# Two-layer hybrid decoder trunk on one core: four projections with the weights as stationary operand, two factors and the skip on VectorE, the state space branch begun a chunk later

## The chip, the core and the metric

The kernel runs on one core of a Trainium2 chip. The core has five engines with an instruction stream each, which meet only through semaphores: TensorE (PE; its weight loads are PEld in the profile), VectorE (DVE), ScalarE (ACT), GpSimd (POOL) and SyncE (SP, which here only issues DMA transfers). An engine works its stream off in the order in which the program was written. Matmuls write to PSUM, eight banks of 512 float32 columns on 128 partitions. The metric is device time of one execution in microseconds.

## What is computed

Sequence 256, width 1024, two layers. Each layer is a gated feed-forward block, a mixer and a second gated feed-forward block, each between two RMS norms and added to the residual h. The mixer, to which the change is confined, is:

```python
q, k, v, z, xbc, dt_raw, u, vg, gate_raw = jnp.split(xn @ w_in, split_at, axis=-1)
y_a = moba_attention(q, k, v)                       # 8 heads x 128, causal, one block of 256
xbc = jax.nn.silu(causal_depthwise_conv(xbc, conv_w, conv_b))
xs, bm, cm = jnp.split(xbc, [SSM_WIDTH, ...])       # 1024, 256, 256 columns
y_s = ssd_scan(xs, dt, a, bm, cm) + d_skip[:, None] * xs
y_s = rms_norm(y_s * jax.nn.silu(z), ssm_norm_g)
u = jax.nn.gelu(u)
vg = layer_norm(jax.nn.gelu(vg), sgu_ln_g, sgu_ln_b)
sv = jnp.einsum('gij,bcjgd->bcigd', tril(sgu_w), vg) + sgu_b   # chunks of 128 tokens
y_c = u * sv
merged = gate0 * (y_a @ p_attn) + gate1 * (y_s @ p_ssm) + gate2 * (y_c @ p_sgu)
return merged @ w_out
```

## The kernel before

**Tiles.** Tokens are two tiles of 128 (t = 0, 1). Activations that feed a large product are kept transposed, features on partitions, in two fp32r parts (hi and lo, `xh` and `xl`). A weight block of 128 x 1024 arrives by DMA (`load`), and `split` makes its two parts: ScalarE casts `whi` (L182), VectorE subtracts for `wlo` (L183). 495 blocks pass so. `done` of a block lets the block 11 places later be split, so a split stands about ten blocks ahead of its use. The RMS factor `r2` of a token is not in x; it is multiplied in where a product leaves PSUM.

**Products.** In `gemm` a 128 x 128 piece of x is the stationary operand and 512 weight columns move: three matmuls per piece, token tile and chunk of 512 columns (L215 xh·whi, L216 xh·wlo, L217 xl·whi), 48 matmuls of 512 columns per chunk. The result has tokens on partitions. Where features are wanted on partitions, ScalarE scales the result out of PSUM (`tokens`, L482), TensorE transposes it in fours (`transposed`, L491, tile `ctr`), and ScalarE copies it out again (L494). This is done for the three chunks of xbc, two of q and two of k. u stays with tokens on partitions; its product y_c is transposed by `to_parts` (L287, `xtr`).

**Order.** One program is written by Python tasks. `pump` is called after each unit of matmuls, advances a clock by their nominal time, steps every task (`tick`) whose wait (table `W`) is over, and then issues one split. What a task issues at a step stands in the streams behind the matmuls issued so far. `finish` steps a task to its end at once. So the order on each engine is fixed by nominal times, not by when things are ready.

**The mixer's sequence** is: xbc (three chunks), z (two), the time steps `dt_task`, q0, then the state space task `ssd` is started; q1, k0, k1, v0, v1 follow, and `finish(ss)`; then attention, the gates and the three output products (`branch`), vg, u, and `sgu` inside the last gates. In `ssd`, for each token tile t and group g: two `weights` steps (matmul `seg` L655, mask add on VectorE L657, four exponentials on ScalarE L661, multiply on VectorE L663), then 8 matmuls `yd` (L686) which need both, and their addition to y and gating by z on VectorE (L689, L697). `scaled` makes y = d_skip·xs on GpSimd (L643) and xs·dt on VectorE (L646).

**Buffers.** PSUM: 5 banks `acc` for the products, 3 banks `tr` for everything else, both handed out in rotation. SBUF: 16 tiles `b4` of 4 KB per partition, 6 tiles `b2` of 2 KB.

Of the kernel before, what the change touches and what calls it, by code (L numbers as in the profile page):

```python
# [17 lines left out]
L = 2  # L18
# [22 lines left out]
G_F1, G_MX, G_F2, G_SSM, G_CW, G_CB, G_SB, G_N = 0, 8, 16, 24, 32, 80, 92, 100  # L41

RAW, SPLIT, HOLD, START, NEAR, PACE = 6, 11, 6, 2, 1, 0
B4, B2 = 16, 6
# [7 lines left out]
def trunk(ctx, tc, a):  # L52
# [49 lines left out]

    sums = cst.tile([P, 512], F32R, name="sums")
    G.memset(sums.bitcast(F32), 0.0)
# [146 lines left out]

    def chunk(key, kt=KD, n=512):
# [56 lines left out]
    class XT:  # L309
# [14 lines left out]
        def l(self, k, t):  # L324
            return self.lo[t][:, k, :]

# [119 lines left out]
    def spatial_weights(l):  # L446
        ws = b4("wsp", (P, 8, P))
        nc.sync.dma_start(ws, a["sgw"][l].rearrange("g j i -> j g i"))
        gb = row("sgu_ln_g", l), row("sgu_ln_b", l)
# [6 lines left out]
    def mixer(l, x, r2, nxt):  # L456
# [11 lines left out]
        halfr, rq = {}, {}  # L468

        def factors():  # L470
            for t in range(NT):
                halfr[t] = small("halfr", 1, bufs=4)
                G.tensor_scalar(halfr[t], r2[t], 0.5, 0.0, op0=ALU.mult, op1=ALU.add)
                rq[t] = small("rq", 1, bufs=4)
                G.tensor_scalar(rq[t], r2[t], float(HD) ** -0.5, 0.0, op0=ALU.mult, op1=ALU.add)

        def tokens(ps, scales, name):

            out = []
            for t in range(NT):  # L480
                o = b2(name)
                A.activation(o, ps[t], AF.Copy, scale=scales[t])  # L482
                out.append(o)
            return out

        def transposed(toks, place, eng):

            for t in range(NT):
                ps = tr("ctr")
                for j in range(4):  # L490
                    T.transpose(ps[:, j * P:(j + 1) * P], toks[t][:, j * P:(j + 1) * P], ident)  # L491
                p3 = ps.rearrange("p (k t) -> p k t", k=4)
                if eng == "a":
                    A.copy(place(t), p3)  # L494
                else:
                    V.tensor_copy(place(t), p3)
                yield W["tr"]
# [6 lines left out]
        def conv(c, ps):  # L504
            toks = tokens(ps, r2, "xtok")
            xc = b4("xc", (P, 4, S))
            yield W["x0"]
            yield from transposed(toks, lambda t: xc[:, :, t * P:(t + 1) * P], "a")
# [32 lines left out]
        def dt_task(wdt):  # L541
# [55 lines left out]
            for j in range(4):  # L597
                T.matmul(pr[:40, j * P:(j + 1) * P], d4[:, j, :], tri, start=True, stop=True)
            A.copy(sums[:40, :], pr[:40, :])
# [12 lines left out]
            st.update(dt=dt, nacs=nacs, eac=eac, dec=dec)  # L612
# [489 lines left out]
```

## Time and profile before

| | us |
|---|---|
| median of three runs | 1508.65 (1508.64 to 1510.26) |
| the profiled execution: its own time | 1512.7 |
| its span, first to last instruction | 1510.9 |
| PE busy in the span | 1496.5 |
| DVE busy, ACT busy | 932.5, 782.7 |
| mean granted TensorE clock | 0.996 |

The profiled execution lies 1.8 us over its span and 4 us over the median of the unprofiled runs. The mixers stand at 205 to 572 us and 955 to 1322 us of the span. TensorE is busy nearly throughout, but a matmul's end in the trace is modelled and its bar overlaps the next, so the distance from one matmul's start to the next one's start is what tells its cost.

### The profile page before, as it was taken

How to read it: one execution, taken by the hardware profiler on the slowest of the kernel's cores; microseconds unless marked ns; L12 is line 12 of the kernel's file. 1: busy time of each engine (PE TensorE's matmuls, PEld its weight loads, DVE VectorE, ACT ScalarE, POOL GpSimd, SP SyncE). 2: the span in 40 equal slices, each digit the busy share in tenths (PEclk: the TensorE clock that was granted, in tenths of full speed). 3: DMA queues.
4: the chain of work that ended last, by engine and by line, in shares of the span. 5: the costliest groups of instructions: out<-in, count | busy, mean ns of one | idle time of the engine just before them, and what ended most of it. 6: DMA issues, size and time to landing. Idle time of an engine off the chain costs nothing.

```text
span 1510.9 us, 18964 instructions
## 1 busy us (share of the span) xinstructions
PE 1496.5 (99%) x7218; PEld 1246.5 (83%) x7218; DVE 932.5 (62%) x1112; ACT 782.7 (52%) x1079; POOL 55.0 (4%) x97
## 2 busy tenths in 40 slices
PE   9999999999999999999999999999999999999998
PEld 7888888878888888888888888888788888888886
DVE  6655468666566858555475554776665677675552
ACT  6544358655374537444364443765554644464441
POOL 0000020000000000000000000200000000100000
PEclk9999999999999999999999999999999999999999
DMA  8766646335556446666566664554354665476650
GB/s 298 251 190 195 195 156 194 124 126 178 158 180 220 172 139 228 199 182 199 154 220 188 182 199 147 210 167 140 112 193 141 195 196 167 154 253 189 186 153 28
DMA packets 77914, 270.29 MB, mean 179 GB/s; under 512 B 8960, under 2 KB 12160, under 8 KB 77824
## 3 DMA queue, kind: packets, MB, share of 16 engines
q1 hardware_dynamic: 77248, 268.76, 55.6%
q8 instruction: 56, 0.92, 0.2%
q10 hardware_dynamic: 576, 0.33, 0.1%
q14 instruction: 34, 0.28, 0.0%
HBM read 268.01 MB, written 1.05 MB: 178 GB/s over the span
## 4 chain that ended last, share of the span: by engine, by line
PE 94%; DVE 4%; ACT 1%; issue 1%; POOL 0%; DMA 0%; DVEq 0%; ACTq 0%; POOLq 0%
PE gu L215 11%; PE gu L217 11%; PE gu L216 11%; PE dn L217 5%; PE dn L216 5%; PE dn L215 5%; PE br L215 3%; PE br L217 3%; PE br L216 3%; PE gate L217 2%; PE gate L215 2%; PE gate L216 2%; DVE wlo L183 2%; PE xbc L215 1%; PE xbc L217 1%; PE xbc L216 1%
## 5 line engine op out<-in xcount | busy, mean ns | idle before, releaser
L183 DVE TENSOR_TENSOR wlo<-raw,whi 128x1024 fp32r<-128x1024 f32 x495 | 601.7, 1234 | 363.0 <-ACT whi L182 362.2
L182 ACT CAST whi<-raw 128x1024 fp32r<-128x1024 f32 x495 | 513.2, 1051 | 380.0 <-PE gu L217 150.6
L215 PE MATMUL gu<-whi,xh 128*128 128x512 f32 (+1 forms) x768 | 291.6, 380 | 1.6 <-ACT xh L303 1.5
L217 PE MATMUL gu<-whi,xl 128*128 128x512 f32 (+1 forms) x768 | 287.1, 374 | 0.0
L216 PE MATMUL gu<-wlo,xh 128*128 128x512 f32 (+1 forms) x768 | 286.7, 373 | 0.0
L217 PEld LDWEIGHTS gu<-whi,xl 128*128 128x128 f32 x768 | 145.3, 189 | 26.8 <-DVE xl L304 1.1
L215 PEld LDWEIGHTS gu<-whi,xh 128*128 128x128 f32 x768 | 145.3, 189 | 26.5 <-ACT xh L303 2.0
L216 PEld LDWEIGHTS gu<-wlo,xh 128*128 128x128 f32 x768 | 145.5, 189 | 24.9 <-DVE wlo L171 0.9
L215 PE MATMUL dn<-whi,hTh 128*128 128x512 f32 x352 | 138.2, 393 | 0.0
L217 PE MATMUL dn<-whi,hTl 128*128 128x512 f32 x352 | 137.1, 390 | 0.0
L216 PE MATMUL dn<-wlo,hTh 128*128 128x512 f32 x352 | 137.1, 389 | 0.0
L217 PEld LDWEIGHTS dn<-whi,hTl 128*128 128x128 f32 x352 | 66.1, 188 | 13.8
L215 PE MATMUL gate<-whi,xh 128*128 128x512 f32 x192 | 77.3, 403 | 0.0
L216 PEld LDWEIGHTS dn<-wlo,hTh 128*128 128x128 f32 x352 | 66.2, 188 | 13.2
L215 PEld LDWEIGHTS dn<-whi,hTh 128*128 128x128 f32 x352 | 66.1, 188 | 13.2
L217 PE MATMUL gate<-whi,xl 128*128 128x512 f32 x192 | 75.0, 390 | 0.0
L216 PE MATMUL gate<-wlo,xh 128*128 128x512 f32 x192 | 74.8, 390 | 0.0
L403 ACT CAST hTh<-htr 128x512 fp32r<-128x512 f32 (+1 forms) x48 | 26.5, 551 | 47.9 <-PE htr L397 47.9
L404 DVE TENSOR_TENSOR hTl<-htr,hTh 128x512 fp32r<-128x512 f32 (+1 forms) x48 | 30.9, 643 | 29.6 <-ACT hTh L403 29.6
L303 ACT CAST xh<-xg 128x512 fp32r<-128x512 f32 (+1 forms) x25 | 15.1, 603 | 62.6 <-DVE xg L301 62.6
L217 PEld LDWEIGHTS gate<-whi,xl 128*128 128x128 f32 x192 | 36.0, 188 | 7.7
L216 PEld LDWEIGHTS gate<-wlo,xh 128*128 128x128 f32 x192 | 36.2, 188 | 6.6
(244 smaller groups left out, 2275.8 us busy)
## 6 DMA issues: line engine op xcount, KB each, us to landing
raw<-in_mix SPq DMA_DIRECT2D x232, 512.0 KB, 4.3
raw<-in_gu SPq DMA_DIRECT2D x175, 512.0 KB, 4.5
raw<-in_dn SPq DMA_DIRECT2D x88, 512.0 KB, 3.7
row_ffn_post_g<-in_ffn_post_g SPq DMA_DIRECT2D x4, 512.0 KB, 4.5
wsp<-in_sgw SPq DMA_DIRECT2D x2, 512.0 KB, 5.3
row_sgu_ln_g<-in_sgu_ln_g SPq DMA_DIRECT2D x2, 512.0 KB, 6.1
row_sgu_ln_b<-in_sgu_ln_b SPq DMA_DIRECT2D x2, 512.0 KB, 7.6
row_mix_post_g<-in_mix_post_g SPq DMA_DIRECT2D x2, 512.0 KB, 6.1
```

The lines of the kernel that those rows point to most:

```text
L182: A.copy(hi, w)
L183: V.tensor_tensor(lo, w, hi.bitcast(F32), op=ALU.subtract)
L215: T.matmul(o, xh(k, t), hi[:, off:off + n], start=first, stop=False)
L216: T.matmul(o, xh(k, t), lo[:, off:off + n], start=False, stop=False)
L217: T.matmul(o, xl(k, t), hi[:, off:off + n], start=False, stop=last)
L303: A.copy(o_h, xg)
L403: A.copy(hi, p3)
L404: V.tensor_tensor(lo, p3, hi.bitcast(F32), op=ALU.subtract)
```

## The change

- `gemm_w` computes xbc, q, k and u with the weights as stationary operand. For each 128 output features and each of 8 input pieces, `whi` (128 x 128) stands while 512 columns move (xh of both token tiles, then xl of both), and `wlo` stands while 256 columns move (xh of both). 64 matmuls per chunk of 512 features: 32 of 512 and 32 of 256 columns. The result has features on partitions; one PSUM bank holds 128 features, hi sum in columns 0 to 255, lo sum in 256 to 511.
- `joined` takes each bank out: ScalarE copies the lo half, VectorE adds the hi half, and after four of them VectorE multiplies all by `rb`, the token factors laid out as a row, which `factor_rows` makes once per layer (two VectorE products with the identity, two matmuls, a copy). `tokens` and `transposed` are gone.
- x lies in one tile (`XW`) so that 512 columns can move; it leaves the `b4` pool, which shrinks from 16 to 12.
- u now has features on partitions: `gelu_columns` replaces `gelu_evac` for it, `sgu` takes vg as stationary operand and writes y_c's parts at once, so that the transposes of y_c are gone; sgu_b comes by a DMA as a row.
- The skip d_skip·xs is made on VectorE. The factor of the state space branch (`rs`) moves from the gate to the merge.
- The sequence is z, then xbc with `dt_task` in it, q0, q1, then `ssd` is started, k0, k1, v0, v1; `finish(ss)` falls away, the branch's own product waits for it.

```diff
+    def gemm_w(n, x, name, out):
...
+        for j in range(n):
+            i = i0 + j
+            need(i)
...
+            hi, lo = parts[i]
+            o = acc(name)
+            for k in range(KD):
+                c = slice(k * P, (k + 1) * P)
+                xk = x.all[:, k].rearrange("p a t -> p (a t)")
+                first, last = k == 0, k == KD - 1
+                pair = [(o, hi, xk, first, last), (o[:, :S], lo, xk[:, :S], False, False)]
+                for dst, w, m, a, z in (pair[::-1] if last else pair):
+                    T.matmul(dst, w[:, c], m, start=a, stop=z)
+                if last:
+                    done(i)
+                    out[j] = o
+                if k % 4 == 3:
+                    pump(1.39)
...
+        def factor_rows():
+
+            ps = tr("rb")
+            for t in range(NT):
+                dg = b2("diag", (P, P))
+                V.tensor_scalar(dg, ident, r2[t], None, op0=ALU.mult)
+                T.matmul(ps[:, t * P:(t + 1) * P], ones, dg, start=True, stop=True)
+            rb[0] = small("rb", S, bufs=1)
+            A.copy(rb[0], ps[:, :S])
+            yield 0
+
+        def joined(o, parts, f=1.0):
+
+            for j in range(4):
+                while j not in parts:
+                    yield 0
+                ps = parts.pop(j)
+                A.copy(o[:, j, :], ps[:, S:])
+                V.tensor_tensor(o[:, j, :], ps[:, :S], o[:, j, :], op=ALU.add)
+            finish(rows[0])
+            V.scalar_tensor_tensor(o, o, f, rb[0][:, None, :].to_broadcast([P, 4, S]), op0=ALU.mult, op1=ALU.mult)
...
             def scaled(t):
 
                 y[t] = b4(f"y{t}")
-                G.tensor_tensor(h3(y[t]), h3(xs[t]), hpar[:, l, 2, :, None].to_broadcast([P, SH, SP]),
+                V.tensor_tensor(h3(y[t]), h3(xs[t]), hpar[:, l, 2, :, None].to_broadcast([P, SH, SP]),
                                 op=ALU.mult)
...
+        def gelu_columns(store, c, parts):
+
+            o = store[c] = b4("u", (P, 4, S))
+            yield from joined(o, parts)
+            x2 = b4("gu2", (P, 4, S))
+            A.activation(x2, o, AF.Square)
+            V.scalar_tensor_tensor(x2, x2, 1.0 / A_GELU, o, op0=ALU.add, op1=ALU.mult)
+            A.activation(x2, x2, AF.Tanh, scale=C_GELU * A_GELU)
+            yield W["ge"]
+            V.scalar_tensor_tensor(o, x2, 1.0, o, op0=ALU.add, op1=ALU.mult)
...
-        cv = []
-        for c, ps in enumerate(project("xbc", head=HOLD, nch=2)):
-            cv.append(spawn(conv(c, ps)))
+        ze = [spawn(z_evac(c, ps)) for c, ps in enumerate(project("z", head=HOLD, nch=2))]
         factors()
-        cv.append(spawn(conv(2, project("xbc")[0])))
-        ze = [spawn(z_evac(c, project("z")[0])) for c in range(2)]
-        finish(*cv)
+        rows = [spawn(factor_rows(), wait=5.2)]
         dte = spawn(dt_task(wdt[l]))
-        at = [spawn(qk_evac("q", 0, project("q")[0]))]
-        finish(dte, *ze)
+        cv = [columns("xbc", conv, c) for c in range(3)]
+        finish(*ze)
+        at = [columns("q", qk_evac, "q", c) for c in range(2)]
+        finish(*cv, dte)
         ss = spawn(ssd(ysx, rs))
-        at.append(spawn(qk_evac("q", 1, project("q")[0])))
         for c in range(2):
-            at.append(spawn(qk_evac("k", c, project("k")[0])))
+            at.append(columns("k", qk_evac, "k", c))
         for c in range(2):
             at.append(spawn(v_evac(c, project("v")[0])))
-        finish(ss)
         finish(*at)
```

The order moves at three places that matter below. First VectorE in the state space branch, from the second multiply of token tile 0, group 0 to the second multiply of group 1 (`ssw` are the weights, `yd` the products, `kT` the keys). Before:

```order
L663 TENSOR_TENSOR ssw<-ssw,cbt 128x512
L183 TENSOR_TENSOR wlo<-raw,whi 128x1024 x3
L689 TENSOR_TENSOR y_2478<-yd,y_2478 128x512
L697 TENSOR_TENSOR y_2478<-y_2478,zs_2157 128x512
L657 TENSOR_TENSOR ssw<-seg,con 128x512
L663 TENSOR_TENSOR ssw<-ssw,cbt 128x512
L657 TENSOR_TENSOR ssw<-seg,con 128x512
```

And now, in the same place:

```order
L713 TENSOR_TENSOR ssw<-ssw,cbt 128x512
L537 TENSOR_TENSOR kT<-k,kT 128x256
L180 TENSOR_TENSOR wlo<-raw,whi 128x1024
L537 TENSOR_TENSOR kT<-k,kT 128x256
L180 TENSOR_TENSOR wlo<-raw,whi 128x1024
L739 TENSOR_TENSOR y_2644<-yd,y_2644 128x512
L747 TENSOR_TENSOR y_2644<-y_2644,zs_1889 128x512
L707 TENSOR_TENSOR ssw<-seg,con 128x512
L713 TENSOR_TENSOR ssw<-ssw,cbt 128x512
L537 TENSOR_TENSOR kT<-k,kT 128x256
L539 SCALAR_TENSOR_TENSOR kT<-kT,rb 128x1024
L180 TENSOR_TENSOR wlo<-raw,whi 128x1024
```

The additions of k and its factor stand between the steps of the branch, and a split between its two multiplies. Next VectorE from the transposes of y's tile 0 (`xg`, `ysl`) to the skip of tile 1. Before:

```order
L301 TENSOR_TENSOR xg<-xtr,par 128x512
L304 TENSOR_TENSOR ysl_2714<-xg,ysh_2713 128x512
L657 TENSOR_TENSOR ssw<-seg,con 128x512
L663 TENSOR_TENSOR ssw<-ssw,cbt 128x512
L646 TENSOR_TENSOR xs_2211<-xs_2211,dt 128x1024
L183 TENSOR_TENSOR wlo<-raw,whi 128x1024
```

Now:

```order
L322 TENSOR_TENSOR xg<-xtr,par 128x512
L325 TENSOR_TENSOR ysl_2870<-xg,ysh_2869 128x512
L707 TENSOR_TENSOR ssw<-seg,con 128x512
L713 TENSOR_TENSOR ssw<-ssw,cbt 128x512
L693 TENSOR_TENSOR y_2921<-xs_2309,hpar 128x1024
L696 TENSOR_TENSOR xs_2309<-xs_2309,dt 128x1024
L180 TENSOR_TENSOR wlo<-raw,whi 128x1024
```

The skip (L693) now stands between the two pairs of weights. Last ScalarE at the end of the branch, where v leaves PSUM. Before:

```order
L661 ACTIVATE ssw<-ssw,nacs 128x128 x4
L494 COPY kT<-ctr 128x4x128
L182 CAST whi<-raw 128x1024
L494 COPY kT<-ctr 128x4x128
L182 CAST whi<-raw 128x1024
L272 ACTIVATE junk,sy<-y_2760 128x1024
L182 CAST whi<-raw 128x1024
L718 ACTIVATE v_2981<-v,r_1684 128x512
L718 ACTIVATE v_2983<-v,r_1761 128x512
```

Now:

```order
L711 ACTIVATE ssw<-ssw,nacs 128x128 x4
L765 ACTIVATE v_3034<-v,r_1678 128x512
L765 ACTIVATE v_3036<-v,r_1753 128x512
L179 CAST whi<-raw 128x1024 x2
L293 ACTIVATE junk,sy<-y_2921 128x1024
```

The v copies now stand ahead of the sum of squares of y and of two casts, and the second of them (`v_3036`) is written into the buffer that xs of tile 1 leaves.

## Rows read from the trace of the kernel before

**Rows 1.** Windows, core 0: us, PE, PEld, DVE, ACT, POOL busy, PEclk, DMA.

```profile
305.30:326.80 21.50, 19.14 (x87) 15.35 (x87) 13.89 (x15) 11.80 (x22) 2.62 (x3) 0.92 0.37 120
317.50:320.90 3.40, 2.69 (x9) 2.33 (x10) 1.99 (x3) 2.69 (x6) 0.00 (x0) 0.50 0.24 96
```

**Rows 2.** Timeline of PE: start us, us, instruction, idle before and releaser.

```profile
316.14 0.49 PE L655 MATMUL seg<-sums,sel 128*128 128x512 f32 x1 [0.79 <-DVE xg L301]
318.21 1.09 PE L491 MATMUL ctr<-con,qtok 128*128 128x128 f32 x4 [1.58 <-DVE ssw L657]
```

**Rows 3.** Timeline of PE: u's first of 96 matmuls, and what follows the last.

```profile
476.04 0.39 PE L215 MATMUL u<-whi,xh 128*128 128x512 f32 x1
...
497.80 0.39 PE L215 MATMUL gate<-whi,xh 128*128 128x512 f32 x1
```

**Rows 4.** Timeline of PE around one group of four transposes, in z.

```profile
240.06 0.40 PE L217 MATMUL z<-whi,xl 128*128 128x512 f32 x1
...
240.65 0.48 PE L215 MATMUL z<-whi,xh 128*128 128x512 f32 x1
240.96 0.40 PE L216 MATMUL z<-wlo,xh 128*128 128x512 f32 x1
```

**Rows 5.** Groups by line and form: count, busy us, mean ns, idle before.

```profile
L183 DVE TENSOR_TENSOR wlo<-raw,whi 128x1024 fp32r<-128x1024 f32 x495 | 601.7, 1234 | 363.0 <-ACT whi L182 362.2
L216 PEld LDWEIGHTS gu<-wlo,xh 128*128 128x128 f32 x768 | 145.5, 189 | 24.9 <-DVE wlo L171 0.9
L491 PE MATMUL ctr<-con,qtok 128*128 128x128 f32 x64 | 10.1, 282 | 3.2 <-DVE ssw L657 3.2
L491 PE MATMUL ctr<-con,xtok 128*128 128x128 f32 x48 | 6.5, 272 | 0.0
L287 PE MATMUL xtr<-con,u 128*128 128x128 f32 x32 | 4.5, 272 | 0.0
L804 DVE SCALAR_TENSOR_TENSOR vg<-vg,mv,row_sgu_ln_g 128x1024 f32<-128x1024 f32 x4 | 5.1, 1285 | 0.1
```

**Rows 6.** Timeline of PE in a feed-forward chunk of 256 columns.

```profile
129.83 0.28 PE L217 MATMUL gu<-whi,xl 128*128 128x256 f32 x1
129.95 0.28 PE L215 MATMUL gu<-whi,xh 128*128 128x256 f32 x1
```

**Rows 7.** Timeline of DVE, the time steps' first and a later operation.

```profile
267.75 0.37 DVE L560 SCALAR_TENSOR_TENSOR dtv<-dtps,r,hpar 128x16 f32<-128x16 f32 x2
...
269.92 1.55 DVE L578 SCALAR_TENSOR_TENSOR dtp<-dtp,dtz 128x32 f32<-128x32 f32 x7
```

**Rows 8.** Timeline of DVE, the branch's gating, mask and multiply.

```profile
293.96 0.69 DVE L697 TENSOR_TENSOR y<-y,zs 128x512 f32<-128x512 f32 x1
294.57 0.68 DVE L657 TENSOR_TENSOR ssw<-seg,con 128x512 f32<-128x512 f32 x1
296.66 0.69 DVE L663 TENSOR_TENSOR ssw<-ssw,cbt 128x512 f32<-128x512 f32 x1 [1.41 <-ACT ssw L661]
```

**Rows 9.** Timeline of ACT behind the exponentials.

```profile
288.27 1.05 ACT L182 CAST whi<-raw 128x1024 fp32r<-128x1024 f32 x1
289.21 0.58 ACT L494 COPY qT<-ctr 128x512 f32<-128x512 f32 x1
```

**Rows 10.** Timeline of DVE from yd's addition to the last multiply before the next yd.

```profile
305.49 0.69 DVE L689 TENSOR_TENSOR y<-yd,y 128x512 f32<-128x512 f32 x1 [0.67 <-PE yd L686]
...
309.12 2.90 DVE L183 TENSOR_TENSOR wlo<-raw,whi 128x1024 fp32r<-128x1024 f32 x1 [2.22 <-ACT whi L182]
...
324.44 0.69 DVE L663 TENSOR_TENSOR ssw<-ssw,cbt 128x512 f32<-128x512 f32 x1 [1.41 <-ACT ssw L661]
```

**Rows 11.** Timeline of POOL in the same stretch.

```profile
309.03 1.91 POOL L643 TENSOR_TENSOR y<-xs,hpar 128x1024 f32<-128x1024 f32 x1
```

**Rows 12.** Timeline of PE at one yd of the branch.

```profile
291.31 1.89 PE L686 MATMUL yd<-xs,ssw 128*128 128x64 f32 x16
293.01 0.48 PE L655 MATMUL seg<-sums,sel 128*128 128x512 f32 x1
```

More of the change, by code (lines that the diff above doesn't have):

```diff
@@ L325, in l, with __init__, new, h @@
             return self.lo[t][:, k, :]
+    class XW:
+        def __init__(self):
+            self.all = None
+        def new(self, t):
+            if self.all is None:
+                self.all = big.tile([P, KD, 2 * NT, P], F32R, name="xw", tag="xw", bufs=1)
+            return self.all[:, :, t, :], self.all[:, :, NT + t, :]
+        def h(self, k, t):
+            return self.all[:, k, t, :]
+        def l(self, k, t):
+            return self.all[:, k, NT + t, :]
     def pre(t, x, r2, gcol, cut, made):
@@ L473, in factors, with columns @@
                 G.tensor_scalar(halfr[t], r2[t], 0.5, 0.0, op0=ALU.mult, op1=ALU.add)
[L474 to L479, printed above, removed]
+        def factor_rows():
+            ps = tr("rb")
             for t in range(NT):
[L481 to L497, printed above, removed]
+                dg = b2("diag", (P, P))
[13 more added lines that the diff above has]
+            V.scalar_tensor_tensor(o, o, f, rb[0][:, None, :].to_broadcast([P, 4, S]), op0=ALU.mult, op1=ALU.mult)
+        def columns(name, task, *args):
+            parts = {}
+            e = spawn(task(*args, parts))
+            gemm_w(4, x.x, name, parts)
+            return e
         xs = {}
@@ L654, in weights @@
                 g = t * 4 + q
[L655 removed]
+                T.matmul(pb, sel[:, g:g + 1].to_broadcast([P, P]), st["sums"], start=True, stop=True)
                 w = b2("ssw", (P, 4, P))
@@ L814, in sgu @@
                         g = 4 * q + j
[L815 removed]
+                        T.matmul(ps[:, j * P:(j + 1) * P], vg[t][:, g * P:(g + 1) * P], ws[:, g, :],
                                  start=True, stop=True)
[L817 to L821 removed]
+                    g4 = slice(4 * q, 4 * q + 4)
+                    v = b2("svb", (P, 4, P))
+                    V.tensor_tensor(v, ps.rearrange("p (g i) -> p g i", g=4), sb[:, g4, :], op=ALU.add)
+                    V.scalar_tensor_tensor(v, v, 0.5, uu[q][:, :, t * P:(t + 1) * P], op0=ALU.mult, op1=ALU.mult)
+                    A.copy(hi[:, g4, :], v)
+                    V.tensor_tensor(lo[:, g4, :], v, hi[:, g4, :].bitcast(F32), op=ALU.subtract)
                     yield W["sv"]
                 yield W["yc"]
[L824 removed]
         merged = {}
@@ L834, in gate_evac, with merge @@
                 if rs is not None:
-                    V.tensor_scalar(g, g, 1.0, rs[t], op0=ALU.add, op1=ALU.mult)
+                    V.tensor_scalar(g, g, 1.0, None, op0=ALU.add)
                 store[c, t] = g
             yield 0
-        def merge(t, slots, ready, store, first, then=None):
-            if first:
+        def merge(t, slots, ready, store, rs, then=None):
+            if rs is not None:
                 merged[t] = b4(f"merged{t}")
@@ L847, in merge @@
                 p1, g = slots[c, t], store[c, t]
-                if first:
-                    V.tensor_tensor(o, p1, g, op=ALU.mult)
+                if rs is not None:
+                    V.scalar_tensor_tensor(o, p1, rs[t], g, op0=ALU.mult, op1=ALU.mult)
                 else:
@@ L856, in merge, with branch @@
                 yield from to_parts(merged[t], *then.new(t))
-        def branch(bx, rs, need, first=False, then=None):
+        def branch(bx, rs, need, then=None):
             store = {}
@@ L871, in on_done @@
                 if t not in out:
-                    out[t] = spawn(merge(t, slots, ready, store, first, then))
+                    out[t] = spawn(merge(t, slots, ready, store, rs, then))
             gemm(chunk(0) + chunk(1), bx.h, bx.l, dst, tail=8 if then is not None else 0, on_done=on_done)
@@ L898, in mixer @@
         att = spawn(attention(yax, free))
-        b0 = branch(ysx, rs, [ss], first=True)
+        b0 = branch(ysx, rs, [ss])
         free.append(True)
```

67 lines of the change are left out of this document (32 added, 35 removed).

## The prediction

> **What bounds the kernel now.** I read the granted clock and the busy times first: TensorE is busy nearly all the span, so every microsecond that leaves its stream or its waits counts. The bars overlap, so I price a matmul by the distance between starts: 96 plain matmuls of 512 columns take 21.76 us, 0.227 each [rows 3]. Then I looked for places where TensorE is not fed. There is one per layer, in the state space branch among k's matmuls. At 316 us `seg` waits 0.79 us for a PSUM bank that VectorE has still to empty, and two instructions later the transposes wait 1.58 us for another [rows 2]. [...] The second layer shows the same two waits. So TensorE bounds the span, but in the branch VectorE and ScalarE bound TensorE: mask (VectorE), exponentials (ScalarE) and multiply (VectorE) alternate in fixed order, and the splits stand between them.
>
> **What TensorE saves.** The transposes behind xbc, q, k and y_c go: 64, 48 and 32 [rows 5], 36 groups of four. With a group between them two matmuls start 0.59 us apart instead of 0.227, and the next distance is 0.31 [rows 4]: 0.44 us a group, 15.8 us in all. The products cost slightly more. A matmul of 256 columns takes 0.12 us from start to start, its own weight load included [rows 6]. A chunk goes from 48 × 0.227 = 10.9 to 32 × (0.227 + 0.12) = 11.1 us; 18 chunks add 3.8. `factor_rows` is priced as a group of four, 0.44 us in each layer, and the transposes of xs stand in four groups instead of two pairs, 0.16 a layer: 1.2 together. TensorE's own work falls by 15.8 − 3.8 − 1.2 = 10.8 us.
>
> [...]
>
> **What the waits cost now.** Before: 0.79 + 1.58 us idle, and of 2.69 us worked at half clock half is lost, 1.35 [rows 1, 2]: 3.7 a layer, 7.4 in all. These I take out and put the new ones in, per layer.
>
> (a) `factor_rows`. TensorE meets its matmuls four pairs, 1.4 us, after the second time-step matmuls. VectorE makes their input after the first eight time-step operations, 2.2 us [rows 7], and two products of about 0.2. With some latency TensorE waits 1.4 us. Ends: 0, and 2.7 if an activation table load falls into it.
>
> (b) Branch, tile 0. From the end of the second exponentials to the next second multiply, in the order of the new stream: ScalarE copies the state (512 columns as the q copy, whose bar is 0.58; I take 0.5), then k copy, cast, k copy, cast. A cast takes 0.94 by starts [rows 9]; a k copy has half the columns of the q copy, I take 0.35. That is 3.1. VectorE follows with a split (1.15 by starts, 1.23 by its bar [rows 5]), addition to y 0.7, gating 0.6, mask to multiply 2.1, multiply 0.6 [rows 8], k addition 0.35 (half the columns of the mask add), factor 1.25 [rows 5], split 1.15, mask to multiply 2.1, multiply 0.7: 13.7 us together. TensorE meanwhile has: 0.7 until the multiply is done, half a yd 0.85 [rows 12], two `seg` and a state product 1.3, 40 matmuls as 20 pairs 6.9, half a yd 0.85: 10.7. (Half a yd, because four of its heads need only the first multiply.) TensorE waits 3.0 us, where it did not wait before. Ends: 0 and 5.
>
> (c) Branch, to tile 1. Before, VectorE needed 19.6 us from the addition of yd to the last multiply [rows 10]. One split in it took 2.90 us while GpSimd made the skip [rows 10, 11], 1.67 over the usual; that goes. New in the chain are the skip on VectorE (1.15, as another product of 1024), the factor of k (1.2) and one of two k additions (0.35), the other fitting into a wait: 20.7. VectorE also reaches the addition 2.65 us after yd's end instead of 0.2, because two k additions and two splits stand ahead of it. TensorE's way from yd's end is 12 pairs 4.2, two groups 0.9, two `seg` 0.6, 48 matmuls of v 10.9, half a yd 0.85: 17.4. It waits 2.65 + 20.7 − 17.4 = 6.0 us, in the place of the old 2.4. Ends: the old 2.4, and 8 if ScalarE adds to it.
>
> (d) The clock falls behind (c) as it did behind 2.4 us idle: 1.35, up to 2.7.
>
> (e) End of the branch. ScalarE's second v copy takes the buffer of xs, so it waits for yd's last matmul; two casts, and so two splits and the last additions of y, queue behind it, and y's transposes wait for those. I take 1.0, ends 0 and 2.5.
>
> (f) u. Its addition, factor and two more passes over 1024 elements make VectorE late at the layer norm of vg. The second product of the gate needs the PSUM bank that VectorE empties then: about 24 us after u's start by the list of its operations, against 23.6. I take 1.0, ends 0 and 2.5. Later, y_c's parts are needed 11 us apart, and that is enough.
>
> xbc and q also load VectorE: 20 splits, 36 convolution steps and 20 additions with five factors come to some 63 us, TensorE's share to 64. PSUM's five banks give 11 us of slack and splits stand ten blocks ahead, so I cost it at nothing; were that cover gone, it would be part of (b). Removing `rs` from the gate and the new row DMA cost nothing: nobody waits for either, raw blocks being loaded far ahead.
>
> (a) to (f) sum to 1.4 + 3.0 + 6.0 + 1.35 + 1.0 + 1.0 = 13.75, 27.5 in two layers.
>
> **The sum.** −10.8 − 7.4 + 27.5 = +9.3 us. On the profiled execution of 1512.7 that is 1522.0; on the median of 1508.65, which lies 4 us lower, it is **1518.0 us**. The gain on TensorE is real, but it falls where TensorE is not the bound.
>
> **Rivals.** (1) VectorE keeps up: k's additions and the skip fill the 1.4 us gaps in which VectorE waits for exponentials, the GpSimd collision is gone, and (b) to (f) come to no more than the old waits. Then −10.8 stays: 1497.9, and 1490.5 if the old waits vanish too. For it: VectorE is busy only 13.9 of 21.5 us there [rows 1]. Against it: the streams are in order, and the additions stand behind the multiplies, not in the gaps. It decides if VectorE's chain in (c) stays under 17.4 us. Chance 0.25. (2) A wash: the new waits come to about 18 us in all, so that gain and loss cancel; 1505.6 to 1511.7. Chance 0.15. (3) Weight loads show when 512 and 256 columns alternate: a load's bar is 0.189 [rows 5], two make 0.378 against 0.347 a pair; 576 pairs add 18 us, 1536. Against it: rows 6. Chance 0.04. [...] Chance 0.08.
>
> **How the numbers follow.** My forecast, 1512 to 1526, has 0.48. About 0.2%, 3 us, is what a measurement of this kernel can tell from no change. Faster is rival 1, 0.25; same is rival 2, 0.15; slower is the forecast with rivals 3 and 4, 0.60. The lower ends of (a) to (f) give 3.75 a layer, 1498; the upper ones 23.4, 1537. The range is 1498 to 1528: it leaves out the lower part of rival 1 and most of rivals 3 and 4.
>
> **What would show it.** Right: no `ctr` rows; 0.347 us a pair in xbc; idle time ahead of yd from VectorE's `ssw` of 3 and 6 us in each layer, and the granted clock at 0.5 behind the latter; 1 to 2 us ahead of `rb`. Wrong: yd follows v's matmuls without idle time (rival 1), or pairs are 0.37 apart (rival 3). The forecast fails most easily if VectorE's and ScalarE's operations overlap better than my sum in (c) lets them.

## The result: 1.7% slower

The changed kernel takes 1535.89 us (median of four runs, 1535.05 to 1536.81) against 1509.45 us for the kernel before in the same runs (1508.64 to 1513.07): a ratio of 1.0169, 95% interval 1.0157 to 1.0181. The forecast was 1518.0 us with a range of 1498 to 1528: the direction was right, and the loss was nearly three times the forecast. The profiled execution of after has its span at 1535.0 us, 24.1 above that of before, and a mean granted clock of 0.989 instead of 0.996. One of the four runs of e4_later below fell into a slower state of the chip (1848 us at a granted clock of 0.753) and is left out of its time.

First the waits of TensorE in the trace of after. The columns are the total over both layers, the number of times and the longest:

```profile
PE qk L782 <- DVE xg L322: 7.3, 2, 3.7
PE yd L736 <- DVE ssw L713: 6.8, 4, 2.7
PE yd L736 <- DVE xs L696: 5.9, 2, 2.9
PE rb L525 <- DVE diag L524: 3.0, 2, 1.5
PE gate L212 <- DVE u L537: 2.8, 2, 1.4
PE state L727 <- DVE y L739: 2.5, 2, 1.3
```

They come to 28.3 us, in the place of the 4.7 of before [rows 2]. The timeline of PE shows them in the first layer (token tile 0 in the first two lines, tile 1 in the next two, then two plain matmuls of v, and the end of the branch in the last):

```profile
304.84 1.12 PE L727 MATMUL state<-xw,btok 128*128 128x512 f32 x2 [1.25 <-DVE y L739]
...
313.58 1.10 PE L736 MATMUL yd<-xs,ssw 128*128 128x64 f32 x8 [1.14 <-DVE ssw L713]
...
334.18 1.94 PE L736 MATMUL yd<-xs,ssw 128*128 128x64 f32 x8 [2.94 <-DVE xs L696]
337.92 1.97 PE L736 MATMUL yd<-xs,ssw 128*128 128x64 f32 x8 [1.80 <-DVE ssw L713]
...
341.93 0.63 PE L212 MATMUL v<-whi,xw 128*128 128x512 f32 x1
342.35 0.63 PE L213 MATMUL v<-wlo,xw 128*128 128x512 f32 x1
...
365.05 2.07 PE L782 MATMUL qk<-kT,qT 128*128 128x128 f32 x8 [3.67 <-DVE xg L322]
```

The two v matmuls start 0.42 us apart, where u before has 0.227 [rows 3]: the granted clock is 0.50 there. The windows of after, read like [rows 1], are the branch of the first layer and then the four stretches of half clock that the two mixers hold:

```profile
282.00:372.00 90.00, 79.21 (x397) 65.83 (x396) 64.74 (x88) 41.57 (x78) 1.49 (x4) 0.91 0.39 127
333.60:343.90 10.30, 7.92 (x24) 6.25 (x25) 7.92 (x11) 3.16 (x6) 0.00 (x0) 0.50 0.48 148
364.40:371.20 6.80, 6.15 (x19) 5.18 (x20) 5.43 (x14) 2.18 (x3) 0.00 (x0) 0.50 0.43 150
1094.80:1101.60 6.80, 5.22 (x14) 3.87 (x15) 5.02 (x6) 2.68 (x5) 0.00 (x0) 0.50 0.58 189
1122.10:1129.00 6.90, 5.81 (x18) 4.94 (x19) 5.53 (x15) 2.33 (x4) 0.00 (x0) 0.51 0.46 152
```

That is 30.7 us at a granted clock of 0.50, behind the waits for yd and behind the wait for qk, where the mixers of before had 6.8 (3.4 at 317.5 us [rows 1] and 3.4 at 1065.0). TensorE is busy 25.1 us in them; by the prediction's estimate (half is lost) that is 12.6 us, against 2.7 before.

On VectorE the chain behind yd's second wait reads as forecast, with the skip (L693) between the two weights of tile 1, and a gap of 1.40 us for the exponentials ahead of the multiply; further down are two waits for ScalarE's casts at the end of the branch, 4.18 and 2.15 us:

```profile
331.56 1.22 DVE L693 TENSOR_TENSOR y<-xs,hpar 128x1024 f32<-128x1024 f32 x1
332.81 1.23 DVE L696 TENSOR_TENSOR xs<-xs,dt 128x1024 f32<-128x1024 f32 x1
333.95 1.22 DVE L180 TENSOR_TENSOR wlo<-raw,whi 128x1024 fp32r<-128x1024 f32 x1
335.08 0.68 DVE L707 TENSOR_TENSOR ssw<-seg,con 128x512 f32<-128x512 f32 x1
337.17 0.69 DVE L713 TENSOR_TENSOR ssw<-ssw,cbt 128x512 f32<-128x512 f32 x1 [1.40 <-ACT ssw L711]
...
354.88 2.36 DVE L180 TENSOR_TENSOR wlo<-raw,whi 128x1024 fp32r<-128x1024 f32 x2 [4.18 <-ACT whi L179]
...
362.04 2.36 DVE L180 TENSOR_TENSOR wlo<-raw,whi 128x1024 fp32r<-128x1024 f32 x2 [2.15 <-ACT whi L179]
364.32 0.68 DVE L322 TENSOR_TENSOR xg<-xtr,par 128x512 f32<-128x512 f32 x1
```

ScalarE says why those casts are late. Its v copy waits for yd's last matmul, which reads the buffer that v gets; then the sum of squares (`junk`) waits for y, and the next casts stand behind it:

```profile
353.22 0.69 ACT L765 ACTIVATE v<-v,r 128x512 f32<-128x512 f32 x1 [2.67 <-PE yd L736]
353.81 1.99 ACT L179 CAST whi<-raw 128x1024 fp32r<-128x1024 f32 x2
359.92 1.06 ACT L293 ACTIVATE junk<-y 128x1024 bf16<-128x1024 f32 x1 [4.13 <-DVE y L747]
```

TensorE's own work did fall, by less than forecast. The first matmul of u and the first one behind u in after:

```profile
486.86 0.39 PE L266 MATMUL u<-xw,whi 128*128 128x512 f32 x1
...
509.42 0.40 PE L212 MATMUL gate<-whi,xw 128*128 128x512 f32 x1
```

64 pairs take 22.56 us, 0.352 each, against 21.76 for u before [rows 3]: 0.40 more per chunk, where 0.21 was taken. Worked out from the start of each product's first matmul to that of the next, the stages of the mixer that moved are, in us (first layer, second layer; e10_all is the last version below):

| stage | before | after | e10_all |
|---|---|---|---|
| xbc, z and q | 89.56, 89.57 | 87.41, 87.35 | 85.65, 85.65 |
| k | 34.13, 34.44 | 32.81, 32.79 | 30.41, 30.47 |
| v | 29.51, 29.54 | 37.56, 37.25 | 30.07, 30.03 |
| first gate | 24.03, 24.04 | 31.78, 31.63 | 26.91, 26.90 |
| u | 21.76, 21.76 | 22.55, 22.55 | 22.55, 22.55 |
| last gate | 27.53, 27.53 | 27.05, 27.02 | 27.02, 27.03 |

The gain stands mainly in the stages ahead of v (3.5 and 3.9 us); v and the first gate, where the branch's longest waits stand, give back more than 15 us in each layer.

### The profile page after: what moved, and what is told of

The parts are those of the page before. It is cut to its first block, busy times and chain, and to the rows that moved or that the text cites. A ratio compares the mean times of both kernels' runs of the same rounds, so it can differ in the third digit from the quotient of the medians.

```text
span 1535.0 us, 19303 instructions
## 1 busy us (share of the span) xinstructions
PE 1496.8 (98%) x7370; PEld 1254.8 (82%) x7370; DVE 978.9 (64%) x1186; ACT 771.8 (50%) x1085; POOL 43.7 (3%) x90
## 4 chain that ended last, share of the span: by engine, by line
PE 86%; DVE 7%; ACT 3%; issue 2%; DMA 2%; POOL 0%; ACTq 0%; DVEq 0%; POOLq 0%; SPq 0%
PE gu L212 10%; PE gu L214 10%; PE gu L213 10%; PE dn L213 5%; PE dn L212 5%; PE dn L214 5%; PE xbc L266 4%; PE q L266 3%; PE gate L212 3%; PE gate L214 3%; PE gate L213 3%; PE br L214 3%; PE br L212 3%; PE br L213 3%; DVE wlo L180 2%
## 5 line engine op out<-in xcount | busy, mean ns | idle before, releaser
L212 PE MATMUL gu<-whi,xw 128*128 128x512 f32 (+1 forms) x768 | 291.0, 379 | 1.4 <-ACT xw L324 0.9
L213 PE MATMUL gu<-wlo,xw 128*128 128x512 f32 (+1 forms) x768 | 286.7, 373 | 0.0
L214 PE MATMUL gu<-whi,xw 128*128 128x512 f32 (+1 forms) x768 | 286.7, 373 | 0.0
L212 PEld LDWEIGHTS gu<-whi,xw 128*128 128x128 f32 x768 | 145.2, 189 | 26.5 <-ACT whi L167 1.6
L214 PEld LDWEIGHTS gu<-whi,xw 128*128 128x128 f32 x768 | 145.2, 189 | 25.8 <-DVE xw L325 0.4
L213 PEld LDWEIGHTS gu<-wlo,xw 128*128 128x128 f32 x768 | 145.3, 189 | 24.9 <-DVE wlo L168 0.9
L212 PE MATMUL gate<-whi,xw 128*128 128x512 f32 x192 | 78.8, 410 | 2.8 <-DVE u L537 2.8
L214 PE MATMUL gate<-whi,xw 128*128 128x512 f32 x192 | 76.4, 398 | 0.0
L213 PE MATMUL gate<-wlo,xw 128*128 128x512 f32 x192 | 76.3, 397 | 0.0
L266 PE MATMUL xbc<-xw,whi 128*128 128x512 f32 x192 | 68.2, 401 | 0.0
L442 ACT CAST hTh<-htr 128x512 fp32r<-128x512 f32 (+1 forms) x48 | 26.5, 552 | 47.2 <-PE htr L436 47.2
L266 PE MATMUL xbc<-xw,wlo 128*128 128x256 f32 x192 | 49.9, 280 | 0.0
L324 ACT CAST xw<-xg 128x512 fp32r<-128x512 f32 (+1 forms) x25 | 15.1, 603 | 64.4 <-DVE xg L322 64.4
```

The lines of the kernel that those rows point to most:

```text
L212: T.matmul(o, xh(k, t), hi[:, off:off + n], start=first, stop=False)
L213: T.matmul(o, xh(k, t), lo[:, off:off + n], start=False, stop=False)
L214: T.matmul(o, xl(k, t), hi[:, off:off + n], start=False, stop=last)
L266: T.matmul(dst, w[:, c], m, start=a, stop=z)
L324: A.copy(o_h, xg)
L442: A.copy(hi, p3)
```

## The experiments

All times are medians; "after" is 1535.89 us. The changed kernel was run only in the first round; the kernel before, run again beside every round of experiments, had medians from 1508.5 to 1510.3 us, so a difference of under 2 us to after is not read as one. The theory: the branch's fixed-order chain through VectorE and ScalarE starves TensorE, and the clock that falls behind each stall lengthens it. The rivals: the waits of single parts (the skip, k's additions, the later start, v's buffer), or a VectorE that is simply full.

### The end of the branch

**e1_v1_own** gives v of tile 1 its own buffer; the ring of raw blocks (`RAW`, the weight blocks as they arrive by DMA) pays for it.

```diff
-RAW, SPLIT, ... = 6, 11, ...
+RAW, SPLIT, ... = 5, 11, ...
...
-                    vv[t] = b4(f"v{t}")
+                    vv[t] = big.tile([P, 1024], F32, name="v1", tag="v1", bufs=1) if t else b4("v0")
```

> The changed kernel, but v of token tile 1 gets a buffer of its own instead of the one that xs of tile 1 leaves (the ring of raw blocks goes from 6 to 5 to make room; loads land 4 us after their issue and stay far ahead). My theory of the end of the branch: ScalarE's v copy waits 2.7 us for yd's last matmul, two casts and two splits queue behind it, the additions of y behind those, and TensorE idles 3.7 us ahead of qk, with a spell of 6.8 us at half clock behind it that costs about 2.7. So the wait ahead of qk should fall under 1 us in each layer and the second spell at 0.50 should go: 2 x (3 + 2.7) = 11 us less than 1535.9, about 1525. Rival: the additions of y are late because VectorE is full, whatever ScalarE waits for; then the wait stays and the time is 1533 to 1537.

Measured 1528.5 us, 7.4 less. The wait ahead of qk fell from 7.3 to 2.4 us, but rb's rose from 3.0 to 4.1, with a new stretch of half clock just behind it in each layer (233.7 to 237.1 and 988.1 to 991.5 us; the mean granted clock of the span is 0.990, where after has 0.989), and xbc took 1.9 and 2.3 us longer: most likely the price of the shorter ring of raw blocks. So the cause was right; the ring's cost is argued from these stages, not measured alone.

**e9_b14** pays with the ring of split blocks (`SPLIT`) instead.

```diff
-RAW, SPLIT, ... = 6, 11, ...
-B4, B2 = 12, 6
+RAW, SPLIT, ... = 6, 10, ...
+B4, B2 = 14, 6
```

> The changed kernel with 14 instead of 12 b4 buffers (the ring of split blocks goes from 11 to 10 to make room), so that v of tile 1 no longer waits for the buffer of xs of tile 1. In e1_v1_own this took the wait ahead of qk from 3.7 to 1.2 us a layer, but the shorter ring of raw blocks there cost about 2.3 us at the end of z in each layer. Theory: without that cost the gain is 10 to 12 us: 1524 to 1526. Rival: splits stand ahead by one block less and bursts at the stages' ends show; then 1528 or more.

Measured 1552.3 us: the rival, and far beyond it. The first wait of its list is one that the list of after doesn't show:

```profile
PE gu L212 <- ACT whi L179: 8.0, 3, 3.1
```

z takes 4.1 us longer in each layer and three of the feed-forward stages 4.7 to 6.6 us, 25.5 together, while v and the first gate get 12.5 back. So one block of lead in 11 is worth some 25 us in this kernel (an estimate: the sum of these five stages; the shorter ring was not run alone). Buffers have to be found elsewhere.

**e12_v_late** moves the copy instead of the buffer.

```diff
                 A.activation(vv[t][:, 512 * c:512 * c + 512], ps[t], AF.Copy, scale=r2[t])
+                if c == t == 0:
+                    yield 9.1
```

> The changed kernel with one line more: ScalarE's copy of v for token tile 1 (first chunk) is issued 9.1 us of nominal time after that of tile 0, behind yd's last matmuls, so that the casts and y's sum of squares no longer queue behind a copy that waits for yd. No ring changes its length. Theory of the end of the branch: the wait ahead of qk falls from 3.7 to about 1.2 us a layer and the second half-clock spell goes or halves: 7 to 11 us less than 1535.9, 1525 to 1529. Rival: the wait ahead of qk comes from VectorE's backlog; then 1533 or more.

Measured 1525.2 us, 10.7 less. Of TensorE's waits the one ahead of qk is all but gone, and the others are as in after:

```profile
PE yd L736 <- DVE ssw L713: 7.0, 4, 2.7
PE yd L736 <- DVE xs L696: 5.9, 2, 2.9
...
PE qk L784 <- DVE xg L322: 0.6, 1, 0.6
```

The half-clock stretches at 364 and 1122 us are gone too; the mean granted clock is 0.993, where after has 0.989. ScalarE's wait, and not VectorE's backlog, made the loss at the end of the branch: 5.3 us a layer, idle time and clock together.

### The clock by itself

**e2_fill** leaves the stall of tile 1 as it is and keeps TensorE busy in it.

```diff
+                        if (t, g) == (1, 0):
+                            half = py if q == 0 else py[:, S:]
+                            for _ in range(12 if q == 0 else 14):
+                                T.matmul(half, x.x.all[:, 0, 0, :], ..., start=True, stop=True)
```

> The changed kernel with TensorE kept busy where it idles ahead of yd of tile 1, group 0: 12 matmuls of 512 columns before its first half and 14 of 256 before its second, into the bank that yd then overwrites, 2.7 and 1.7 us of work in the place of 2.9 and 1.8 us idle. The stall itself stays. Theory: the granted clock falls because TensorE idles there, and the spell of 10.2 us (first layer) and 6.8 us (second) at 0.50 costs half of the work done in it, 4.0 and 2.6 us; so 6.6 us less, about 1529, and no spell at 0.50 there, while the second spell, behind the wait ahead of qk, stays. Rival: the fall has another cause, or the time is not limited by the clock there since VectorE sets the pace; then 1534 to 1538.

Measured 1531.6 us, 4.3 less. In the stretch where after had 0.50, the columns being those of [rows 1]:

```profile
333.60:343.90 10.30, 10.30 (x59) 8.72 (x58) 8.46 (x11) 3.18 (x7) 0.00 (x0) 1.00 0.47 146
```

So with TensorE kept busy ahead of yd the granted clock is 1.00 there, and matmuls that compute nothing bring 4.3 us back. Half-clock time in the mixers fell from 30.7 to 13.6 us (the mean granted clock of the span is 0.994 for the 0.989 of after; new stretches of 3.4 us came at 315 and 510 us, and those behind the wait for qk, which stays, are 3.4 instead of 6.8 us), and 17 us less of it gave 4.3. Half of this time would be an estimated 8.5 us; the measurement is half of that. Two things in the traces make the difference. TensorE worked only 25.1 of the 30.7 us of after, but nearly all of the 13.6 left here, so by the prediction's estimate, half of the work and not of the time, 5.8 us go. And TensorE waits longer elsewhere: 1.0 us more ahead of the gate (2.8 in after), and 0.5 us in each layer ahead of yd of tile 1, group 1, where after has no wait.

```profile
PE gate L212 <- DVE u L537: 3.8, 2, 2.1
```

### Which part of the change makes the stall ahead of yd

**e3_skip_pool** undoes the skip.

```diff
-                V.tensor_tensor(h3(y[t]), h3(xs[t]), hpar...
+                G.tensor_tensor(h3(y[t]), h3(xs[t]), hpar...
```

> The changed kernel with one part undone: the skip is made on GpSimd again. Theory: VectorE's chain ahead of yd of tile 1 loses 1.2 us for the skip, but one split runs beside GpSimd's product and is 1.7 us longer, as it was before; the chain is as long as now, so 1533 to 1539, with yd's wait of 4.7 to 5.6 us in each layer still there. Rival: the skip on VectorE is the cause of the stall; then the waits of yd for xs (2.9 in each layer) go, and with them part of the half-clock spells: 1523 to 1528.

Measured 1534.9 us, as expected. VectorE's chain is 1.2 us shorter, and one split becomes 1.4 us longer just while GpSimd works (one row of POOL, one of DVE):

```profile
320.51 1.91 POOL L693 TENSOR_TENSOR y<-xs,hpar 128x1024 f32<-128x1024 f32 x1
```

```profile
320.87 2.63 DVE L180 TENSOR_TENSOR wlo<-raw,whi 128x1024 fp32r<-128x1024 f32 x1 [0.52 <-ACT whi L179]
```

The same split takes 1.23 us in after, where no GpSimd product runs beside it; here it takes 2.63, beside a product of 1.91. In before, too, a split beside such a product is longer than the others [rows 10, 11]. By what the product lengthens it was not shown.

**e8_k_bare** and **e14_k_bare_pool** take k's additions off VectorE, and then the skip too (e14 has the edit of e3_skip_pool beside this one). k is then its hi half alone, without its factor.

```diff
+            if which == "k":
+                for j in range(4):
+                    while j not in parts:
+                        yield 0
+                    A.copy(qk[which, c][:, j, :], parts.pop(j)[:, :S])
+                return
```

> The changed kernel without VectorE's part of k: its eight additions of the halves and two factors per layer are left out (k is the upper half alone, unscaled, so the output isn't the reference's); ScalarE's eight copies stay, and TensorE's work is the same. It takes 5.2 us of work per layer off VectorE within the branch. Theory: k's additions lengthen VectorE's chain in the branch, so the waits ahead of yd and state in tile 0 (2.7 a layer) go and those in tile 1 fall by about 2, the first half-clock spells get shorter; the wait ahead of qk stays: 1520 to 1527. Rival: k's additions fit into VectorE's gaps; then 1532 to 1536.

> As e8_k_bare (k is the upper half alone, unscaled, so the output isn't the reference's) with the skip on GpSimd again: of the work that the change adds to VectorE in the branch nothing is left. Theory A (VectorE's added work makes the stall): the waits ahead of yd and state fall from 6.8 a layer to the 2.4 of before; the wait ahead of qk and its spell stay: 1520 to 1525. Theory B (the later start, or what else stands there, makes it): they stay above 5 a layer, 1529 to 1533, about e8_k_bare.

Measured 1531.5 and 1529.9 us: 4.4 and 6.0 less; e8 lies above its theory's range and just below its rival's, e14 in that of theory B. In e14 nothing is left on VectorE of what the change put between the steps of the branch; only q's last addition and factor still stand just behind its start, 1.6 us. TensorE still waits (both layers, trace of e14):

```profile
PE yd L736 <- DVE ssw L713: 5.6, 4, 2.7
PE yd L736 <- DVE xs L696: 3.5, 2, 1.7
...
PE state L727 <- DVE y L739: 0.8, 2, 0.4
```

That is 9.9 us instead of 15.2, though before had 4.7: between the two theories. What was taken off VectorE makes 5.3 of the 10.5 us by which the stall grew, half.

**e13_early** undoes the later start.

```diff
-        at = [columns("q", qk_evac, "q", c) for c in range(2)]
+        at = [columns("q", qk_evac, "q", 0)]
         finish(*cv, dte)
         ss = spawn(ssd(ysx, rs))
+        at.append(columns("q", qk_evac, "q", 1))
```

> The changed kernel with one part undone: the state space branch begins after the first chunk of q again, so it runs beside q1, k and v0. Theory A (VectorE's added work makes the stall, wherever the branch stands, since q's and k's additions are alike): the waits ahead of yd and state stay at 7 to 9 us a layer; the wait ahead of qk (3.7) goes, since v's copies then come after the branch; the steps of the last convolution are forced and cost 1 to 3 us ahead of cb: 1525 to 1530. Theory B (the later start makes the stall): the waits ahead of yd fall under 3 us a layer as well: 1512 to 1520.

Measured 1534.0 us, near after and above both theories. The wait ahead of qk is gone, and a new one takes its place, for the last convolution, which `finish` now forces earlier:

```profile
PE btr L584 <- ACT conv L569: 6.1, 2, 3.0
```

The waits ahead of yd and state are 15.8 us where after has 15.2. So it isn't the later start either: theory A holds for where the waits stand.

What is left is TensorE itself. From `cb`, the branch's first matmuls, to the first yd of tile 1 the trace of before has these rows, and after has `cb` at 287.73:

```profile
277.23 0.94 PE L632 MATMUL cb<-conv 128*128 128x128 f32 x7
...
326.79 1.89 PE L686 MATMUL yd<-xs,ssw 128*128 128x64 f32 x16
```

```profile
287.73 1.05 PE L682 MATMUL cb<-conv 128*128 128x128 f32 x8
```

TensorE's own way, without its waits, was 49.56 − 0.79 − 1.58 − 1.35 (clock) = 45.8 us; now it is 46.45 − 1.25 − 1.14 − 2.94 = 41.1. VectorE's, from `cb` to the end of the last multiply that yd needs and with its own waits in it, was 47.9 [rows 10] and is 50.1. The gap between them grew from 2.1 to 9.0 us: 4.7 because TensorE got faster, 2.2 because VectorE got slower. In e14 VectorE's way is 47.2, what it was before, and TensorE still waits. Of the saved transposes six groups stood in just this stretch, 2.6 us at the prediction's price, and they were what TensorE did while VectorE's chain ran. No run gave TensorE this work back, so this half of the stall's growth is worked out from rows and not shown by an experiment.

**b1_pairs** asks whether the kernel before suffers from the same chain (its edit is that of e5_pairs below).

> The kernel before with nothing but the order of e5_pairs in the branch (both masks, both exponentials, xs x dt, both multiplies; the skip stays on GpSimd). Theory: in the kernel before the same in-order round trips make its waits ahead of seg and of ctr (2.4 us a layer) and its half-clock spells (1.35 a layer), so these go: 1502 to 1507. Rival: they come from the split that runs beside GpSimd's product, or from the banks; then 1508 to 1511.

Measured 1511.5 us, ratio 1.0018 (1.0009 to 1.0027): the rival, half a microsecond above its range. The wait only moved:

```profile
PE ctr L491 <- DVE xg L301: 4.9, 2, 2.5
```

The transposes of k wait for a bank that VectorE empties, in either order of the weights (1.58 us in before [rows 2], 2.5 here). A VectorE chain that is shorter was worth nothing there. Whether VectorE empties that bank late because of the split beside GpSimd's product, which stands ahead of it, was not run.

### The order

**e4_later** moves yd down TensorE's stream (with v's own buffer as in e1_v1_own).

```diff
-                    yield W["w2"]
+                    yield W["w2"] + {(0, 0): 1.95, (0, 1): 1.3, (1, 0): 6.5, (1, 1): 0}[t, g]
```

> As e1_v1_own, and TensorE's yd stands later in its stream: 2.0, 1.3 and 6.5 us of nominal time more between the second weights and yd for tile 0 group 0, tile 0 group 1 and tile 1 group 0. Same work on every engine, only the order changes. Theory: the loss is made by the order, TensorE meets yd before the chain of VectorE and ScalarE is through, though other matmuls are at hand. Then the waits ahead of yd (5.2 a layer), state (1.3) and qk (3.7) mostly go and with them all half-clock spells (11.7): about 1504 to 1512, faster than before. Rival: VectorE as a whole has too little room in the branch, and the waits come back later, ahead of the gate's or the branch product's matmuls: 1520 or more.

Measured 1522.0 us (1520.4 to 1526.5), 6.5 less than e1_v1_own where 16 to 24 were expected. The waits ahead of yd are gone, but others come up later, ahead of the next `seg` and of the transposes `xtr`, as the rival foresaw:

```profile
PE seg L705 <- DVE y L739: 5.6, 2, 2.8
...
PE xtr L308 <- DVE rden L799: 4.0, 2, 2.0
```

Moving the reader alone doesn't shorten the chain.

**e5_pairs** shortens the chain: both masks, then both sets of exponentials, with the skip and xs·dt in VectorE's gap.

```diff
                     weights(t, 2 * g)
+                    weights(t, 2 * g + 1)
                     if g == 0:
                         scaled(t)
-                    yield W["w1"]
-                    weights(t, 2 * g + 1)
+                    weighed(t, 2 * g)      # the multiply, taken out of weights
+                    weighed(t, 2 * g + 1)
...
-                    yield W["w2"]
+                    yield W["w1"] + W["w2"]
```

> The changed kernel with the two weights of a group made together: both seg matmuls, both mask additions, both sets of exponentials, then (in group 0) the skip and xs x dt, then both multiplies; the same operations, and the waits before yd in TensorE's stream keep their nominal length. Theory: VectorE loses 1.41 us before each multiply waiting for ScalarE's exponentials, in order, although other work is at hand; with the work put into those gaps its chain from the first mask addition to the second multiply of tile 1, group 0 falls from 9.0 us to about 5, so yd's waits (5.2 a layer in tile 1, 1.4 in tile 0) mostly go, and the first half-clock spell of each layer with them (4.0 and 2.6). The wait ahead of qk behind v's copy stays. About 19 less than 1535.9: 1513 to 1521. Rival: VectorE is short of throughput, not held up by the round trips; then the waits only move, 1528 or more.

Measured 1517.6 us, 18.3 less, as expected. The waits ahead of yd are gone from the list, the one ahead of qk stays, and a smaller one ahead of `seg` is new:

```profile
PE qk L785 <- DVE xg L322: 7.4, 2, 3.7
...
PE seg L705 <- DVE y L742: 2.8, 2, 1.4
```

**e6_pairs_diag** makes rb's inputs before the time steps, beside the edit of e5_pairs.

```diff
+            dg = [b2("diag", (P, P)) for t in range(NT)]
+            for t in range(NT):
+                V.tensor_scalar(dg[t], ident, r2[t], None, op0=ALU.mult)
+            yield 5.2
             ps = tr("rb")
...
-        rows = [spawn(factor_rows(), wait=5.2)]
+        rows = [spawn(factor_rows())]
+        step(rows[0])
```

> As e5_pairs, and factor_rows makes its two VectorE products (diag) at once when z is through, 5.2 us of nominal time ahead of their matmuls, so that they no longer stand behind the eight time-step operations on VectorE. Theory: TensorE's 1.5 us ahead of rb in each layer go and nothing takes their place: 3 us less than e5_pairs, 1510 to 1518. Rival: TensorE then waits 1 us or more for something else there, and the time is that of e5_pairs within 1 us.

Measured 1514.3 us, 3.3 less than e5_pairs; xbc went from 41.11 to 39.36 us.

**e10_all** adds to e6_pairs_diag the late v copy of e12_v_late and a gap between two `seg`.

```diff
+                    if t == g == 1:
+                        yield W["w1"]
                     weights(t, 2 * g + 1)
```

> e6_pairs_diag with the late v copy of e12_v_late, and with 1.3 us of nominal time between the two seg matmuls of tile 1, group 1 (there the second waits 1.4 us for the bank of yd in e6). Theory: each wait has its own cause and they add up. e6 still loses 3.7 a layer ahead of qk with a half-clock spell in one layer (2.7), and 1.4 a layer ahead of seg; about 10 less than 1514.3: 1501 to 1508, faster than before by 0.2 to 0.6%, since TensorE's own work is less than before. Rival: y's chain at the end of the branch is bound by VectorE as well; then 1511 or more.

Measured 1504.6 us (1504.16 to 1505.27): 0.9967 of before, interval 0.9955 to 0.9978. This version beats both kernels. VectorE's chain for tile 1 now has no gap, and the granted clock is 1.00 throughout the branch (rows of DVE, then the window with the columns of [rows 1]):

```profile
322.72 1.28 DVE L709 TENSOR_TENSOR ssw<-seg,con 128x512 f32<-128x512 f32 x2
323.92 1.22 DVE L695 TENSOR_TENSOR y<-xs,hpar 128x1024 f32<-128x1024 f32 x1
325.17 1.23 DVE L698 TENSOR_TENSOR xs<-xs,dt 128x1024 f32<-128x1024 f32 x1
326.31 1.29 DVE L718 TENSOR_TENSOR ssw<-ssw,cbt 128x512 f32<-128x512 f32 x2
```

```profile
280.00:360.00 80.00, 77.58 (x418) 64.31 (x418) 64.63 (x89) 42.60 (x84) 1.48 (x4) 1.00 0.45 146
```

From the first mask to the last multiply it is 4.9 us, where after has 9.0 (328.85 to 337.86). The single gains, 18.3 (order), 3.3 (diag) and 10.7 (v copy), sum to 32.3; together with the gap they gave 31.3. So the stalls have separate causes in the main. The sum isn't exact: 3.3 us of waiting ahead of qk are back, where e12_v_late has 0.6.

**e11_all_ln** tries the layer norm ahead of the last gate: `'ln': 10.4` becomes `'ln': 5.2`.

> As e10_all, and the second token tile of the layer norm of vg follows the first after 5.2 instead of 10.4 us of nominal time, so that on VectorE it stands ahead of u's last additions less closely. Theory: TensorE's 1.4 us a layer ahead of the third gate's second bank come from u's additions standing behind that layer norm; 1 to 3 us less than e10_all. Rival: the sum of VectorE's work there is what counts, not its order: the same as e10_all within 1 us.

Measured 1504.6 us, the same; the wait ahead of that gate is 2.8 us in both traces. The time is the rival's: where the layer norm stands doesn't matter. That the sum of VectorE's work makes this wait was argued and not tested.

## Why the prediction was right and wrong

**The direction and the reason** were right: the gain on TensorE fell where TensorE isn't the bound, and the branch turned it into stalls. The runs bear it out: e5_pairs, e6_pairs_diag and e12_v_late take the stalls away one by one, and e10_all, without them, is faster than before.

**(a) `factor_rows`.** 1.5 us a layer for 1.4. e6_pairs_diag shows its reason: 3.3 us when VectorE makes the input early.

**(b) and (c), the branch.** 2.4 (1.25 and 1.14) for 3.0, and 4.7 (2.94 and 1.80) for 6.0 in the first layer, 2.4 and 5.6 in the second: sizes and places right, a little high. Their working put the skip and k's additions in front. The runs give these half of what the stall grew by (e14); the rest is, by the rows under e13_early, mostly TensorE's own shorter way, which the sum had in it (17.4 us for its way in (c)) and the words didn't say.

**(d) The clock, the step that failed most.** I took the one spell of before, 3.4 us at a granted clock of 0.50 [rows 1], as 1.35 us a layer with an end of 2.7. After has two spells in each layer, of 6.8 to 10.2 us, 12.6 us by my own estimate where 2.7 were in the sum. The number was carried over from a wait of 2.4 us to one of 4.7 us and to one at the end of the branch, without a row that showed either; for the one at the end of the branch the sum had nothing. Keeping TensorE busy in the stalls at yd gave 4.3 us (e2_fill), with two new spells elsewhere counted against it.

**(e) The end of the branch.** The mechanism was named (the v copy waits for yd, casts and splits queue behind it) and mis-sized: 3.7 us for 1.0, beyond the end of 2.5. The sum stopped at one wait for ScalarE; the trace has three in a row, v copy 2.67, splits 4.18, sum of squares 4.13, each released by another engine. e12_v_late puts the whole at 10.7 us in two layers with its clock.

**(f) u.** 1.4 for 1.0, within its ends.

**TensorE's savings.** A pair costs 0.352 us, not 0.347, and a chunk 0.40 more than before, not 0.21: 18 chunks add 7.2 instead of 3.8, so 7.4 us are saved, not 10.8. Rival 3 was wrong all the same: it added up two load bars of 0.189 us, but in the trace of after the loads start 0.12 and 0.23 us apart, so their bars overlap. If each of the 288 extra loads had shown in full, with its bar of 0.189 us [rows 5], that would have been an estimated 54 us. 7.2 us is all that the pairs cost more, so the trace shows most of this time hidden.

**From the profile to the median.** The 4 us taken off belonged in part to the one execution of before: it holds a stretch of half clock near its start, where after has 1.00.

```profile
20.60:24.00 3.40, 3.40 (x9) 2.65 (x8) 2.77 (x3) 3.40 (x7) 1.09 (x3) 0.50 0.57 194
```

Half of 3.4 us is 1.7; the profiled execution of after lies only 0.9 over its median.

The sum with measured terms: 28.3 − 4.7 idle, 12.6 − 2.7 − 1.7 clock, − 7.4 work = +24.4 us, against 24.1 between the spans (the clock by the estimate that half is lost, and 1.2 of the work still as the prediction took it). That is 15.1 above the forecast's 9.3: 9.9 of it are (d), 5.3 are (e) and 3.4 TensorE's own work, against 2.8 that (b) and (c) came out lower; the other terms come to 0.7 less. The range ended at 1528 because rival 4 (upper ends and a longer spell, 1526 to 1537) was given 0.08; its time and its longer spell are what happened, but of its upper ends only that of (e) was reached.

Not settled: why the stretches at half clock are 3.4 us long in one place and 10.2 in another. And the later start could only be undone in the changed kernel (e13); the kernel before with the later start wasn't run.

## What to carry to other kernels

Before taking work off the bounding engine, find what runs beside that work on the others: where a chain through two in-order engines was hidden under it, the saving can come back as a stall (here the one ahead of yd and state grew by 10.5 us), so cost the chain against the engine's new, shorter way. Try two stages that alternate between VectorE and ScalarE in pairs, with other work in the gaps; that order was worth 18 us here, in the kernel whose TensorE had become faster, and nothing in the one before. Price the clock behind a stall from a row with a stall of that length; where no row has one, say so and leave the range open on that side.

## What the runs showed of the hardware

- A pair of matmuls of 512 and 256 columns, each with its own weight load, takes 0.352 us: 0.234 and 0.118 from start to start in u of the first layer. 64 such matmuls in the place of 48 of 512 columns, which had a load each as well, cost TensorE 4% more (22.56 for 21.76 us).
- Filling TensorE's idle time with matmuls that compute nothing made the kernel 4.3 us faster (e2_fill); the granted clock was 1.00 from 333.6 to 343.9 us instead of 0.50.
- One block less in the ring of eleven split blocks made the kernel 16 us slower, although the two b4 buffers that it paid for shortened the wait ahead of qk from 7.3 to 3.5 us (e9_b14).
